# Moving the load of the decay floors' logits to the end of the first tile's chains of loads and remainders

## Chip, cores and metric

The kernel runs on one core of a Trainium2 chip. The metric is the device time of one execution in microseconds (us). The change concerns a stretch of some 40 us at the start of an execution of about 1.86 ms.

A core has a matrix engine (TensorE, PE in the profile; its weight loads are shown apart as PEld), a vector engine (VectorE, DVE), a scalar engine (ScalarE, ACT), GpSimd (POOL) and SyncE (SP), which here issues most of the DMA transfers. Each of them works through its own list of instructions in order. Where an instruction has to wait, all that stands behind it in that list waits too.

## The reference

A decoder trunk of two layers over 512 tokens of width 1024. Each layer adds three branches to the residual stream x:

```python
for l in range(DEPTH):
    x = x + 0.5 * swiglu(rms_norm(x, ffn1_norm[l]), ffn1_w_in[l], ffn1_w_out[l])
    h = rms_norm(x, mix_norm[l]) @ w_mix_in[l]
    ...
    x = x + y @ w_mix_out[l]      # y: short convolution, HGRN2 and forgetting attention side by side
    x = x + 0.5 * swiglu(rms_norm(x, ffn2_norm[l]), ffn2_w_in[l], ffn2_w_out[l])
```

The HGRN2 heads of the middle branch have a learned lower bound (floor) for their decay. The floors of both layers come from a softmax over the layers of a small array of logits, 2 x 256 numbers:

```python
lb_soft = jax.nn.softmax(hgrn_lb_logits.astype(jnp.float32), axis=0)
lower_bounds = jnp.clip(jnp.cumsum(lb_soft, axis=0) - lb_soft[0:1], 0.0, 1.0)
```

The floors are first needed in layer 0's middle branch, whose first instruction that reads them (L1201) starts 373.2 us into the profiled execution.

## The kernel before

**Products in three passes.** Every float32 operand is split into a high part (`hi`), written by ACT as a rounded copy, and a remainder (`lo`), which DVE computes as the operand less its high part. A product is three matmuls: high by high, high by remainder, remainder by high.

**The opening** (`open_stream`, L1546 to L1649) is the first tile of the first feed-forward branch: columns 0 and 1 of the gate and of the up projection, so four accumulators, over eight slices j of 128 input features, taken in pairs k = 0, 2, 4, 6. For each slice:

- `load(j)` (L1554) has SP fetch 256 KB of x into `xs`; `weights(k)` (L1572) has SP fetch 512 KB of weights for a pair of slices into `st`, of which there are two buffers. So the weights of k = 4 can only be issued when those of k = 0 have been split.
- `turn(j)` (L1562) turns the slice with four PE transposes into a PSUM bank.
- `norm_part(j, ..., 0)` multiplies by the norm's gain: ACT writes the high part of the activations (L381), DVE the remainder (L382).
- `part` (L1579) splits the weights: ACT the high part (L1581), DVE the remainder (L1582).
- `product` (L1625) issues the matmuls, twelve for each slice: four accumulators by three passes.
- The bank is copied to the residual stream by DVE (L1647), and squares are summed for the norm, by ACT (L392, L395) and DVE (L396).

For k = 0 the twelve products of slice 0 come first, then those of slice 1, accumulator by accumulator. Slices 2 and 3 are turned between the two groups.

**What sets the order.** The builder arranges the instructions of each engine by itself, by priority and by its own estimate of when each can run. Where the kernel wants a certain order it calls `follow(engine, instruction)` (L273). This keeps one chain for each engine, "p" (PE), "a" (ACT), "v" (DVE), "s" (SP) and "g" (POOL), and adds a dependence on the last instruction in the chain, which costs no semaphore but fixes which of the two comes first on their engine. In the opening all loads are in chain "s" (two are in ACT's "a"), all high parts in "a", all remainders in "v", all transposes and products in "p". What is not in a chain is placed by the builder wherever it sees room.

**After the opening**, in `cover` (L481), come `build_consts` (masks, by DVE at L231 to L241; the builder pulls much of this forward into the opening), the sum of squares through PE (`end_norm`, L408) with its logarithm, exponential and square on ACT (L413, L414 and L401, all shown as L267, the line of the helper `act`) and three steps on DVE (L402 to L404), then `lower_bounds` (L918), the procedure that the change touches. It fetches the logits (L930), copies the first layer's row (L932), takes the maximum (L934), subtracts it (L937), has ACT take the exponential (L938, shown as L267 on tile lb), normalises, sums and clips (L940 to L967) and has ACT take a logarithm (L970). ACT then loads another table of functions (L258), which waits in ACT's list behind all of these.

The second tile (f = 2) follows at once. Its weights are fetched by L287, whose instructions are in chain "s", behind the loads of the opening, and split at L304 (ACT) and L305 (DVE). Its fourth accumulator is the bank that `end_norm` has used.

Of the kernel before, what the change touches and what calls it, by code (L numbers as in the profile page):

```python
# [23 lines left out]
P = 128  # L24
# [132 lines left out]
class Trunk:  # L157
# [760 lines left out]
    def lower_bounds(self, logits, scratch):  # L918
        nc = self.nc
        used = 0  # L920

        def take(*shape):
            nonlocal used
            n = shape[0] * (shape[1] if len(shape) > 1 else 1)
            t = scratch[:, used : used + n]
            used += n
            return t.rearrange("p (l r) -> p l r", r=2) if len(shape) > 1 else t

        lg = take(DEPTH, 2)
        nc.sync.dma_start(lg, logits.rearrange("l (r p) -> p l r", p=P))  # L930
        m = take(2)
        nc.vector.tensor_copy(m, lg[:, 0, :])  # L932
        for l in range(1, DEPTH):
            nc.vector.tensor_max(m, m, lg[:, l, :])  # L934
        e = take(DEPTH, 2)
        for l in range(DEPTH):
            nc.vector.tensor_sub(e[:, l, :], lg[:, l, :], m)  # L937
        self.act(e, e, AF.Exp)  # L938
        s = take(2)
        nc.vector.tensor_copy(s, e[:, 0, :])  # L940
        for l in range(1, DEPTH):
            nc.vector.tensor_add(s, s, e[:, l, :])
        nc.vector.reciprocal(s, s)
        for l in range(DEPTH):
            nc.vector.tensor_mul(e[:, l, :], e[:, l, :], s)
        self.lb = self.const.tile([P, DEPTH, 2], F32, tag="lb", name="lb")

        self.lb1 = self.const.tile([P, DEPTH, 2], F32, tag="lb1", name="lb1")
        cum = take(2)
        nc.vector.tensor_copy(cum, e[:, 0, :])  # L950
        for l in range(DEPTH):
            if l:
                nc.vector.tensor_add(cum, cum, e[:, l, :])
            d = take(2)
            nc.vector.tensor_sub(d, cum, e[:, 0, :])
            nc.vector.tensor_scalar(
                self.lb[:, l, :], d, scalar1=0.0, scalar2=1.0, op0=ALU.max, op1=ALU.min
            )
            nc.vector.tensor_scalar(
                self.lb1[:, l, :], self.lb[:, l, :], scalar1=-1.0, scalar2=1.0,  # L960
                op0=ALU.mult, op1=ALU.add,
            )
        one = take(DEPTH, 2)
        nc.vector.tensor_scalar(
            one, self.lb1, scalar1=0.0, scalar2=-1e30, op0=ALU.is_equal, op1=ALU.mult
        )
        nc.vector.tensor_scalar(  # L967
            self.lb1, self.lb1, scalar1=2.0**-40, scalar2=None, op0=ALU.max
        )
        self.act(self.lb1, self.lb1, AF.Ln)  # L970
        nc.vector.tensor_add(self.lb1, self.lb1, one)
# [729 lines left out]
```

## Time and profile before

| | |
|---|---|
| timed runs, median of 3 | 1856.22 us |
| lowest and highest timed run | 1854.98 and 1859.03 us |
| the profiled execution's own time | 1863.95 us |
| its span in the trace | 1862.1 us |
| PE busy | 1842.6 us, 99% of the span |
| DVE, ACT, POOL busy | 1480.4, 1003.3, 177.4 us |
| DMA traffic | 251.91 MB, mean 135 GB/s |

The profiled execution is one single execution, recorded instruction by instruction. The timeline lists instructions with their start, their duration, and in brackets how long their engine had been idle before them and what ended that wait. Consecutive like instructions are merged into one row with their count (x5). Durations of consecutive instructions overlap a little, since an engine starts one before the end of the last is recorded; the distance between starts is then the pace. The chain of waits goes back from the end and shows at each point of time what the end depended on. The granted clock of PE is a column in the views by stretches of time: 1.00 is full speed.

### The profile page before, as it was taken

The numbers are of one execution on the slowest core, as the hardware profiler recorded it, in microseconds if no ns is written. First come the engines' busy times: TensorE is split into PE (matmuls) and PEld (weight loads), VectorE is DVE, ScalarE is ACT, GpSimd is POOL, SyncE is SP. The second block draws the span as 40 slices with busy tenths as digits, with TensorE's granted clock in tenths as the row PEclk, the third lists the DMA queues.
The fourth block names the chain that finished last, engine by engine and source line by source line (L and its number), as shares of the span: only waits on it lengthen the run. The fifth ranks groups of instructions, "written<-read, shape, count | busy, mean of one in ns | idle before, by whom it ended". The sixth has DMA issues, their size and how long they took to land.

```text
span 1862.1 us, 33406 instructions
## 1 busy us (share of the span) xinstructions
PE 1842.6 (99%) x13551; PEld 1712.6 (92%) x13551; DVE 1480.4 (80%) x2102; ACT 1003.3 (54%) x1465; POOL 177.4 (10%) x182
## 2 busy tenths in 40 slices
PE   8999999999999999999999999999999999999998
PEld 7899999899878899999889999998998788999997
DVE  8889787677887888878678887876768878888883
ACT  5455554564675454545445555555546665555552
POOL 0011120100000001112001111201000000021210
PEclk9999999999999999999999999999999999999999
DMA  5858783332323756868265787823323238577662
GB/s 162 212 121 195 176 179 91 74 93 69 80 80 93 213 134 156 183 168 171 80 194 132 163 178 188 166 69 76 90 68 86 76 97 226 146 156 197 147 138 91
DMA packets 244427, 251.91 MB, mean 135 GB/s; under 512 B 18569, under 2 KB 229009, under 8 KB 244273
## 3 DMA queue, kind: packets, MB, share of 16 engines
q1 hardware_dynamic: 190512, 183.56, 32.7%
q0 software_dynamic: 53600, 66.09, 22.3%
q8 instruction: 106, 1.74, 0.4%
q14 instruction: 49, 0.39, 0.1%
q10 hardware_dynamic: 160, 0.14, 0.0%
HBM read 223.98 MB, written 2.10 MB: 121 GB/s over the span
## 4 chain that ended last, share of the span: by engine, by line
PE 89%; DVE 6%; ACT 2%; issue 1%; DMA 1%; SPq 0%; ACTq 0%; DVEq 0%
PE mm L315 13%; PE mm L322 13%; PE mm L321 13%; PE sc L322 6%; PE sc L315 6%; PE sc L321 6%; PE pt L315 6%; PE pt L321 6%; PE pt L322 6%; PE po L315 3%; PE po L322 3%; PE po L321 3%; PE po L1477 1%; PE pt L1518 1%; DVE hl L305 1%
## 5 line engine op out<-in xcount | busy, mean ns | idle before, releaser
L771 ACT CAST hl<-w 128x1024 fp32r<-128x1024 f32 x322 | 337.1, 1049 | 327.6 <-PE mm L322 77.2
L773 DVE TENSOR_TENSOR hl<-w,hl 128x1024 fp32r<-128x1024 f32 x322 | 392.8, 1222 | 93.2 <-ACT hl L771 93.0
L305 DVE TENSOR_TENSOR hl<-st,hl 128x512 fp32r<-128x512 f32 (+2 forms) x188 | 161.4, 859 | 115.3 <-ACT hl L304 114.3
L304 ACT CAST hl<-st 128x512 fp32r<-128x512 f32 (+2 forms) x188 | 142.0, 755 | 184.3 <-PE mm L322 70.7
L315 PE MATMUL mm<-xc,hl 128*128 128x256 f32 (+1 forms) x732 | 202.3, 277 | 1.8 <-ACT g L877 1.4
L321 PE MATMUL mm<-xc,hl 128*128 128x256 f32 x728 | 202.0, 277 | 0.0
L322 PE MATMUL mm<-xc,hl 128*128 128x256 f32 x728 | 202.0, 277 | 0.0
L315 PE MATMUL sc<-xc,hl 128*128 128x256 f32 (+1 forms) x530 | 147.1, 278 | 2.5 <-ACT g L877 1.7
L322 PE MATMUL sc<-xc,hl 128*128 128x256 f32 x528 | 146.8, 278 | 0.0
L321 PE MATMUL sc<-xc,hl 128*128 128x256 f32 x528 | 146.7, 278 | 0.0
L315 PEld LDWEIGHTS mm<-xc,hl 128*128 128x128 f32 x732 | 137.3, 188 | 2.5 <-ACT g L877 1.8
L321 PEld LDWEIGHTS mm<-xc,hl 128*128 128x128 f32 x728 | 137.4, 189 | 0.0
L322 PEld LDWEIGHTS mm<-xc,hl 128*128 128x128 f32 x728 | 136.7, 188 | 0.1
L315 PE MATMUL pt<-xc,hl 128*128 128x256 f32 (+1 forms) x484 | 133.6, 277 | 0.0
L321 PE MATMUL pt<-xc,hl 128*128 128x256 f32 x480 | 133.4, 278 | 0.0
L322 PE MATMUL pt<-xc,hl 128*128 128x256 f32 x480 | 133.2, 278 | 0.0
L315 PE MATMUL mm<-hl,x 128*128 128x256 f32 (+1 forms) x384 | 112.3, 293 | 0.7 <-DVE qk L1408 0.3
L315 PE MATMUL mm<-x,hl 128*128 128x512 f32 x272 | 109.3, 402 | 0.0
L322 PE MATMUL mm<-hl,x 128*128 128x256 f32 (+1 forms) x384 | 107.4, 280 | 0.0
L321 PE MATMUL mm<-hl,x 128*128 128x256 f32 (+1 forms) x384 | 107.2, 279 | 0.0
L322 PE MATMUL mm<-x,hl 128*128 128x512 f32 x272 | 106.9, 393 | 0.0
L321 PE MATMUL mm<-x,hl 128*128 128x512 f32 x272 | 106.0, 390 | 0.0
(490 smaller groups left out, 5689.8 us busy)
## 6 DMA issues: line engine op xcount, KB each, us to landing
w<-in_ffn_w_in_dram SPq DMA_DIRECT2D x140, 512.0 KB, 5.3
w<-in_ffn_w_out_dram SPq DMA_DIRECT2D x64, 512.0 KB, 4.5
w<-in_ffn_w_out_dram POOLq DMA_DIRECT2D x56, 512.0 KB, 8.7
st<-in_w_mix_in_dram SPq DMA_DIRECT2D x88, 256.0 KB, 2.7
st<-in_ffn_w_in_dram SPq DMA_DIRECT2D x70, 256.0 KB, 3.5
w<-in_ffn_w_in_dram POOLq DMA_DIRECT2D x35, 512.0 KB, 8.7
w<-S POOLq DMA_DIRECT2D x35, 512.0 KB, 4.7
st<-in_ffn_w_out_dram SPq DMA_DIRECT2D x24, 512.0 KB, 3.5
```

The costliest lines, as they stand in the source:

```text
L304: a = nc.scalar.copy(hi, src[:, c : c + w])
L305: b = nc.vector.tensor_sub(lo, src[:, c : c + w], hi)
L315: i = nc.tensor.matmul(acc[:, c], ah, bh[:, c], start=first and c.start == 0, stop=False, skip_group_check=True,)
L321: nc.tensor.matmul(acc, ah, bl, start=False, stop=False, skip_group_check=True)
L322: i = nc.tensor.matmul(acc, al, bh, start=False, stop=last, skip_group_check=True)
L771: A(nc.scalar.copy(hi, src))
L773: return lambda: V(nc.vector.tensor_sub(lo, src, hi))
L1477: nc.tensor.matmul(self.ob[:, t0 + u * P : t0 + 2 * P], V[:, j, h % 4].rearrange("p a d -> p (a d)"), part[:, j, u:, :].rearrange("p i t - ...
L1518: nc.tensor.transpose(tb[:, j * P : (j + 1) * P], p[:, j * P : (j + 1) * P], self.ident)
```

## The change

```diff
         lg = take(DEPTH, 2)
-        nc.sync.dma_start(lg, logits.rearrange("l (r p) -> p l r", p=P))
+        self.follow("s", nc.sync.dma_start(lg, logits.rearrange("l (r p) -> p l r", p=P)))
         m = take(2)
-        nc.vector.tensor_copy(m, lg[:, 0, :])
+        self.follow("v", nc.vector.tensor_copy(m, lg[:, 0, :]))
         for l in range(1, DEPTH):
             nc.vector.tensor_max(m, m, lg[:, l, :])
```

When `lower_bounds` is called, the last link of chain "s" is the load of the opening's last pair of weights (k = 6), and the last link of chain "v" is the weight remainder of slice 7. So the transfer of the logits is placed on SP behind all loads of the opening, and the copy on DVE behind all its remainders. The steps that read the copy's result (L934 on) come later with it. What joins the two chains afterwards, the loads of the second tile first of all, comes behind them. No instruction is added or taken away, and nothing that is computed changes.

## Prediction

> **What bounds the kernel now.** I read the page's engine table first, then the chain of waits over the opening.
>
> ```profile
> span 1862.1 us, 33406 instructions
> PE 1842.6 (99%) x13551; PEld 1712.6 (92%) x13551; DVE 1480.4 (80%) x2102; ACT 1003.3 (54%) x1465; POOL 177.4 (10%) x182
> ```
>
> ```profile
> 7.68 4.87 DMA lb<-in_hgrn_lb_logits_dram
> ...
> 13.98 2.67 PE sc L1625 x5
> 16.65 2.56 PE pt L1625 x6
> 19.21 1.75 PE sc L1625 x6
> 20.96 1.37 PE pt L1625 x6
> 22.32 0.87 PE mm L1562 x8
> ```
>
> PE sets the time nearly everywhere. The exception is early: from 7.68 us the end depends on a transfer of 2 KB, the logits. The timeline of DVE, then of PE, shows who stood behind it.
>
> ```profile
> 8.16 0.22 DVE L231 TENSOR_SCALAR c<-c 128x128 f32<-128x128 f32 x1
> 12.57 0.17 DVE L932 COPY lb<-lb 128x2 f32<-128x2 f32 x1 [4.20 <-DMA lb<-in_hgrn_lb_logits_dram]
> 12.65 0.28 DVE L233 TENSOR_TENSOR c<-c,c 128x128 f32<-128x128 f32 x1
> 12.85 0.15 DVE L934 TENSOR_TENSOR lb<-lb 128x2 f32<-128x2 f32 x1
> 12.97 0.29 DVE L234 TENSOR_TENSOR lmask<-c,c 128x128 uint8<-128x128 f32 x1
> 13.18 0.74 DVE L382 SCALAR_TENSOR_TENSOR x<-mm,gain,x 128x512 fp32r<-128x512 f32 x1
> 13.84 0.68 DVE L1582 TENSOR_TENSOR hl<-st,hl 128x512 fp32r<-128x512 f32 x1
> ...
> 16.57 0.68 DVE L1582 TENSOR_TENSOR hl<-st,hl 128x512 fp32r<-128x512 f32 x1
> ```
>
> ```profile
> 10.47 0.48 PE L1625 MATMUL sc<-x,hl 128*128 128x512 f32 x1
> 13.98 0.80 PE L1625 MATMUL sc<-x,hl 128*128 128x512 f32 x1 [3.03 <-DVE x L382]
> ```
>
> DVE stands still for 4.20 us at the copy L932. Slice 1's activation remainder (L382) is behind it, and PE has done one of slice 1's twelve products and waits for that remainder. The pause has a second cost, which the stretches of half a microsecond show (columns: stretch, its length, PE, PEld, DVE, ACT, POOL busy, granted PE clock, DMA share, GB/s):
>
> ```profile
> 12.00:12.50 0.50, 0.00 (x0) 0.00 (x0) 0.00 (x0) 0.00 (x0) 0.00 (x0) 1.00 0.16 1
> 13.00:13.50 0.50, 0.00 (x0) 0.00 (x0) 0.50 (x3) 0.00 (x0) 0.00 (x0) 0.54 0.00 0
> 19.00:19.50 0.50, 0.50 (x3) 0.40 (x2) 0.50 (x2) 0.35 (x1) 0.00 (x0) 0.50 0.55 162
> 20.00:20.50 0.50, 0.50 (x4) 0.41 (x3) 0.50 (x2) 0.41 (x1) 0.00 (x0) 1.00 0.96 252
> ```
>
> PE's last product before the pause ends at 10.95. From about 13.0 the granted clock is 0.50, and it is 1.00 again only after 19.5. Products done meanwhile run at half pace.
>
> **The change, part by part.** *The pause removed.* The chain's row at 20.96, at full clock, gives the pace: six products in 1.37 us, 0.23 each. After the product at 10.47 the next could start at 10.70; it started at 13.98. That is **3.28 us**. *The half clock removed.* The chain's three pieces from 13.98 on are 17 products in 2.67 + 2.56 + 1.75 = 6.98 us; at 0.23 they take 3.91. That is **3.07 us**. Together 6.35, if nothing else is late.
>
> What is late next? ACT's part of slice 1 (timeline of ACT) is early:
>
> ```profile
> 8.02 0.69 ACT L381 ACTIVATE x<-mm,gain 128x512 fp32r<-128x512 f32 x1 [1.72 <-PE mm L1562]
> 8.61 0.61 ACT L1581 CAST hl<-st 128x512 fp32r<-128x512 f32 x1
> ```
>
> L382 can start at 8.71; if DVE fills in L233 and L234 first, at about 8.9. So DVE's list moves up by 13.18 - 8.9 = 4.3 us, and ends slice 1's weight remainder near 10.2 (14.52 before). PE needs these at 10.70 and 10.93, both there. Slice 2: PE arrives at 10.70 + 11 x 0.23 = 13.2 and needs the weight remainder at 13.7; it was ready at 17.25, so now near 12.95. Slice 3 comes after twelve products (2.76) and the transposes (0.87 at 22.32), from 16.8; its two large DVE steps follow those of slice 2 and have 3 us more. The smallest margin is 0.7 us; an order of DVE that puts one more operation of 0.7 us ahead costs nothing, a second one its length. The later slices hang on PE's own transposes, and move with PE.
>
> Do the transfers keep up? The row at 12.00 shows 1 GB/s: all that had been issued has landed, the x slices 4 and 5 included, which PE now turns at 16.0. The remaining loads wait on SP for buffers, not for the wire:
>
> ```profile
> 14.55 0.88 SPq L1572 DMA_DIRECT2D st<-in_ffn_w_in_dram  x2
> ...
> 18.54 0.88 SPq L1572 DMA_DIRECT2D st<-in_ffn_w_in_dram  x2
> 26.16 13.97 SPq L287 DMA_DIRECT2D st<-in_ffn_w_in_dram  x8
> ```
>
> The weights of slices 4 and 5 (14.55) waited for slice 1's remainder, ended 14.52; so they go near 10.3, and those of 6 and 7 (18.54) some 4.3 earlier too. Slice 4 is turned at 22.32 and multiplied after that, so its weights had 7.8 us or more from their issue. They now go 4.3 earlier and are wanted 6.3 earlier, which leaves 5.8. The longest landing of this stretch that I have quoted, behind a full queue, is the logits' 4.87.
>
> *The transfer moved.* It is one issue on SP. It stood at 7.68, after which SP waited until 14.55 anyway, and goes behind the row of 18.54, which ends at 19.42, ahead of the row of 26.16: SP has 6.7 us there and pays nothing. It landed 4.87 after issue behind a full queue; issued near 15 it is there by 20. The copy cannot run before slice 7's weight remainder, which ends at 34.2 (33.55 + 0.68) in the next rows, near 27.9 when 6.3 are taken off. So the copy finds its data, unless the transfer takes 13 us.
>
> *The copy and what follows it.* L932 and L934 (0.32 together) leave a pause and enter a busy stretch of DVE. Then comes the one place without slack:
>
> ```profile
> 33.55 0.68 DVE L1582 TENSOR_TENSOR hl<-st,hl 128x512 fp32r<-128x512 f32 x1
> ...
> 35.35 0.16 DVE L940 COPY lb<-lb 128x2 f32<-128x2 f32 x1
> ...
> 36.21 0.69 DVE L396 TENSOR_TENSOR sqa<-sqa,sq 128x512 f32<-128x512 f32 x1
> ```
>
> ```profile
> 40.51 0.19 ACT L267 ACTIVATE lb<-lb 128x4 f32<-128x4 f32 x1
> 40.64 0.63 ACT L267 ACTIVATE nr<-nr 128x512 f32<-128x512 f32 x1
> ```
>
> ```profile
> 42.71 0.19 PEld L315 LDWEIGHTS po<-x,hl 128*128 128x128 f32 x1 [0.40 <-DVE nt L402]
> ```
>
> The floors' logarithm (40.51) stands on ACT ahead of the norm's exponential (40.64) and square; L402 on DVE takes the square; PE's fourth accumulator of the second tile waits for L402, already 0.40. If the floors come x later, PE waits up to x more. Lower bound 0: from 34.2 the copy, maximum and exponential fit before L940 at 35.35. Upper bound, if DVE takes its larger steps first: the copy goes behind L396, which ends at 36.9 (36.21 + 0.69), 1.55 after L940's old place. I take **0.35**, near the lower end, since the copy's turn comes with the next gap of DVE. Sum: 6.35 - 0.35 = **6.0 us**.
>
> The profiled execution would have a span of 1862.1 - 6.0 = 1856.1 and a time of 1857.95, as 1.85 lay around its span before. Its own time is 7.73 above the median of the runs, so I subtract from the median: 1856.22 - 6.0 = **1850.2**, with 1848.5 to 1852 for this case alone: 1.2 more for the full 1.55 on the floors and 0.6 for one margin overdrawn; the other way the 0.35, and up to 1.3 for the waits on DVE inside the slow pieces of the chain, which shrink too.
>
> The Trainium skill ("TensorE: Matmul & The Clock Gate", Part 1: The HAM clock gate) says that PE falls to half clock after an idle window of about 3.4 us and recovers after about 3.4 us of busy work, in a window that runs freely. By that rule the half clock would cost about 1.7 us and the sum would be near 4.6; the rows show the clock down after some 2 us of pause and for more than 6 us, so they don't agree in length, and the rows are what I use.
>
> **Rivals.** *The pause does not cost the clock in timed runs.* The profile is slower than the median by more than I expect to win, and may hold a slow stretch that they lack. Then only 3.28 - 0.35 = 2.9 is won: 1853.3. For it: those 7.73 us, and that the pause is short, 3.03. Against: the pause follows from an order, which all runs share. By the freely running window of the Trainium skill ("TensorE: Matmul & The Clock Gate", Part 1) it would be a matter of chance in each execution; one profile can't show that.
>
> *The floors come late (slower).* Place: ACT's list ahead of the norm. If the builder puts the exponential there while DVE does the copy only behind the second tile's third weight remainder:
>
> ```profile
> 40.05 1.23 DVE L305 TENSOR_TENSOR hl<-st,hl 128x1024 fp32r<-128x1024 f32 x1 [0.35 <-ACT hl L304]
> ```
>
> then the floors start from 41.28, need 0.6 to the exponential and the 5.16 from 35.35 to 40.51: 47.0, 6.5 late. PE pauses 6.5, and pays the 3.07 of half clock again: 9.6 - 6.35 = 3.2 slower, 1859.4. It decides from a lateness of 6.35 - 3.07 = 3.3. Against: L940 ran at 35.35 between two large steps, and the copy can do so too.
>
> *The builder arranges later stages differently.* Every moved estimate can change its choices.
>
> ```profile
> 42.00:1862.10 1820.10, 1805.27 (x13392) 1682.31 (x13390) 1447.42 (x2002) 982.68 (x1430) 176.34 (x174) 1.00 0.56 135
> ```
>
> PE idles 14.8 us in all the rest. Twice that costs 14.8 - 6.0 = 8.8: 1865; it decides from 6.0. A third less wins 5 more: 1845. For it: the middle branches have few chains. Against: that idle time is small and scattered.
>
> *It does not do what it says:* another wait ends the same pause, 1856. Only slice 1's inputs could, and their rows are early.
>
> **How the numbers follow.** Forecast 0.55; clock rival 0.15; late floors 0.05; other arrangement 0.22 (0.08 better, 0.04 in between, 0.10 worse); no effect 0.03. With 0.2% (3.7 us, about what a measurement tells from no change): faster 0.55 + 0.08 + 0.05 of the clock rival = 0.68; slower 0.10 + 0.02 = 0.12; same 0.20. The range, 1846.5 to 1857.5, leaves out most of the worse arrangements and late floors (0.13) and the best arrangements (0.05).
>
> **What would show it.** In the profile after: no idle row of 4 us on DVE before L932; L382 of slice 1 near 8.9; PE without a pause from 6.4 to 40 and a granted clock of 1.00 from 10 to 20; twelve products in about 2.8 us; the transposes of slices 4 and 5 near 16 instead of 22.32; the fourth accumulator's first product near 36.7 instead of 42.71; 14.8 us of idle PE later as before. It is wrong if PE pauses near 11 for something else, if the clock is at half with no pause, or if the 6 us are won by 40 us and gone at the end.

## The result and the profile after

| | before | after |
|---|---|---|
| timed runs, median | 1858.03 us (22 runs) | 1853.42 us (22 runs) |
| lowest and highest | 1853.8 and 1863.9 | 1849.17 and 1860.92 |
| ratio of after to before | | 0.9974, 95% interval 0.9962 to 0.9985 |
| second measurement (e12 below) | 1859.16 us (12 runs) | 1852.91 us (7 runs), ratio 0.9964, 0.9947 to 0.9982 |
| span of the profiled execution | 1862.1 us | 1853.6 us |

The change makes the kernel faster, by 0.26% in the first measurement and 0.36% in the second. The forecast of 6.0 us is a ratio of 0.9968, inside both intervals. But 4.6 us between the first medians, 6.2 between the second, and 8.5 between two profiled spans are three different answers, and single runs of one kernel spread over 10 us. (One of the twelve runs of e5 below took 3720.07 us, twice the others, for a reason that nothing here shows; it stands in no ratio.) So the opening is read by a mark inside it: the start of **the first product of the second tile's fourth accumulator** (L315 on tile po), 42.71 us before.

The chain of waits of the changed kernel, over the stretch that was shown of before (start, duration, what):

```profile
10.30 0.44 PE po L1562 x4
10.74 1.39 PE sc L1625 x6
12.13 1.36 PE pt L1625 x6
13.49 1.36 PE sc L1625 x6
14.85 1.36 PE pt L1625 x6
16.21 0.87 PE mm L1562 x8
```

The transfer of the logits is gone from it, and PE goes through without a break. Slices 4 and 5 are turned from 16.21 instead of 22.32: 6.11 us earlier. The 18 products of the three pieces from 10.74 take 4.11, so 17 take 3.88 where they took 6.98: 3.10 us are the slow products, and the other 3.01 are the pause. (By the starts in the timeline of PE the second product of slice 1 comes at 10.81 instead of 13.98, so 3.17 are the pause, and some 2.93 are left for the products; the expectations below use this split.) The timeline of DVE after shows why:

```profile
8.16 0.22 DVE L231 TENSOR_SCALAR c<-c 128x128 f32<-128x128 f32 x1
8.41 0.29 DVE L233 TENSOR_TENSOR c<-c,c 128x128 f32<-128x128 f32 x1
8.73 0.29 DVE L234 TENSOR_TENSOR lmask<-c,c 128x128 uint8<-128x128 f32 x1
8.94 0.75 DVE L382 SCALAR_TENSOR_TENSOR x<-mm,gain,x 128x512 fp32r<-128x512 f32 x1
9.61 0.68 DVE L1582 TENSOR_TENSOR hl<-st,hl 128x512 fp32r<-128x512 f32 x1
```

The copy L932 has left its place between L231 and L233. Slice 1's remainder L382 starts at 8.94 (13.18 before). SP's list and the norm's steps on ACT (timelines), and the mark:

```profile
14.31 0.88 SPq L1572 DMA_DIRECT2D st<-in_ffn_w_in_dram  x2
15.23 0.47 SPq L930 DMA_DIRECT2D lb<-in_hgrn_lb_logits_dram  x1
20.04 7.18 SPq L287 DMA_DIRECT2D st<-in_ffn_w_in_dram  x3
```

```profile
34.53 0.20 ACT L267 ACTIVATE lb<-lb 128x4 f32<-128x4 f32 x1
34.64 0.62 ACT L267 ACTIVATE nr<-nr 128x512 f32<-128x512 f32 x1
```

```profile
36.70 0.50 PE L315 MATMUL po<-x,hl 128*128 128x512 f32 x1
```

The mark comes at 36.70, 6.01 us earlier. Of the 6.11 won by 16.21 us only 0.10 is lost on the way to it.

### The profile page after: what moved, and what is told of

Read it like the earlier page. It is cut to its first block, busy times and chain, and to the rows that moved or that the text cites. A ratio compares the mean times of both kernels' runs of the same rounds, so it can differ in the third digit from the quotient of the medians.

```text
span 1853.6 us, 33407 instructions
## 1 busy us (share of the span) xinstructions
PE 1836.2 (99%) x13551; PEld 1707.7 (92%) x13551; DVE 1480.4 (80%) x2102; ACT 1002.6 (54%) x1465; POOL 177.3 (10%) x182
## 4 chain that ended last, share of the span: by engine, by line
PE 90%; DVE 6%; ACT 3%; issue 1%; DMA 0%; ACTq 0%; DVEq 0%
PE mm L315 13%; PE mm L322 13%; PE mm L321 13%; PE sc L322 6%; PE sc L315 6%; PE sc L321 6%; PE pt L315 6%; PE pt L321 6%; PE pt L322 6%; PE po L315 3%; PE po L321 3%; PE po L322 3%; PE po L1477 1%; PE pt L1518 1%; DVE hl L305 1%
## 5 line engine op out<-in xcount | busy, mean ns | idle before, releaser
L315 PE MATMUL mm<-xc,hl 128*128 128x256 f32 (+1 forms) x732 | 201.6, 276 | 1.8 <-ACT g L877 1.4
L315 PE MATMUL sc<-xc,hl 128*128 128x256 f32 (+1 forms) x530 | 147.1, 278 | 2.5 <-ACT g L877 1.7
L315 PEld LDWEIGHTS mm<-xc,hl 128*128 128x128 f32 x732 | 137.2, 188 | 2.5 <-ACT g L877 1.8
L315 PE MATMUL pt<-xc,hl 128*128 128x256 f32 (+1 forms) x484 | 133.6, 277 | 0.0
L315 PE MATMUL mm<-hl,x 128*128 128x256 f32 (+1 forms) x384 | 112.6, 293 | 1.3 <-DVE zf L1073 0.6
L315 PE MATMUL mm<-x,hl 128*128 128x512 f32 x272 | 109.2, 402 | 0.0
```

The source lines that it names most:

```text
L315: i = nc.tensor.matmul(acc[:, c], ah, bh[:, c], start=first and c.start == 0, stop=False, skip_group_check=True,)
```

## The experiments

**e1 and e2: each half of the change alone.**

```diff
 e1
-        nc.vector.tensor_copy(m, lg[:, 0, :])
+        self.follow("v", nc.vector.tensor_copy(m, lg[:, 0, :]))
 e2
-        nc.sync.dma_start(lg, logits.rearrange("l (r p) -> p l r", p=P))
+        self.follow("s", nc.sync.dma_start(lg, logits.rearrange("l (r p) -> p l r", p=P)))
```

> Only the copy is in its chain; the transfer stays where it was, early on SP. The mark is the first product of the second tile's fourth accumulator (42.71 us before, 36.70 with the whole change). Theory (what counts is what stands behind the copy on DVE): mark 36.7, no pause of PE, granted clock 1.00 from 10 to 20 us, time as with the whole change, about 5 to 6 us under before. Rival (the early transfer itself holds up the loads behind it on SP or in the queue): the mark stays over 38.

> Only the transfer is in its chain; the builder places the copy by its own estimate, which comes out behind slice 5's remainders. Theory: the copy finds its data there, mark 36.7 and time as with the whole change. Rival (the builder's estimate of the landing is too early here as well): DVE waits 1 to 4 us before the copy near 23 us, and the mark lies between 37.5 and 41.

Measured: e1 1851.24 us against 1858.71, ratio 0.9951 (0.9931 to 0.9972); e2 1852.58, ratio 0.9965 (0.9946 to 0.9984). The marks, e1 first:

```profile
36.86 0.50 PE L315 MATMUL po<-x,hl 128*128 128x512 f32 x1 [0.15 <-DVE nt L402]
```

```profile
36.68 0.50 PE L315 MATMUL po<-x,hl 128*128 128x512 f32 x1
```

Either half alone does what both do. In e1 the transfer is still issued early, and holds up nobody: only the copy's place on DVE matters. In e2 the builder knows that the transfer is late and puts the copy behind slice 5's remainders by itself, where it does not wait (timeline of DVE, e2):

```profile
22.86 0.22 DVE L232 TENSOR_SCALAR c<-c 128x128 f32<-128x128 f32 x1
23.00 0.16 DVE L932 COPY lb<-lb 128x2 f32<-128x2 f32 x1
23.12 0.29 DVE L233 TENSOR_TENSOR c<-c,c 128x128 f32<-128x128 f32 x1
```

e1 shows one more thing. The floors' logarithm starts at 34.69 in it, 0.16 later than after the whole change, and the mark is 0.16 later:

```profile
34.69 0.21 ACT L267 ACTIVATE lb<-lb 128x4 f32<-128x4 f32 x1
34.80 0.62 ACT L267 ACTIVATE nr<-nr 128x512 f32<-128x512 f32 x1
```

So the place without slack that the prediction named is real: there, lateness of the floors goes one for one into PE.

**e4, e6, e7: the pause brought back without the logits.** All have the whole change, and fillings on DVE in the place of the old wait (ten, six and fourteen).

```diff
-        zeros = fp.tile([P, T], F32, tag="u2", name=self.n("z"), bufs=2)[:, :P]
+        wide = fp.tile([P, T], F32, tag="u2", name=self.n("z"), bufs=2)
+        zeros = wide[:, :P]
...
                     turn(1)
+                    for _ in range(10):
+                        V(nc.vector.memset(wide, 0.0))
                     make(1)
```

> The whole change, with ten fillings of a 128x512 tile with zeros added on DVE ahead of slice 1's activation remainder, about 4.4 us of DVE's time where the wait was. No logits are involved. Theory: the old pause comes back with its half clock, PE pauses 3.2 us, the mark is 42.7 to 42.9, the time as before. Rival (the half clock came from the stretch of DMA traffic or was chance): PE pauses 3.2 us, but the clock stays at 1.00 and the mark is 39.9.

> The whole change with six fillings on DVE ahead of slice 1's activation remainder (ten gave a pause of 4.13 us on PE, 0.66 each). Theory (the clock falls only after a pause of some length): pause 1.5, clock 1.00 throughout, mark 36.70 + 1.5 = 38.2. Rival (each microsecond of pause costs its share of clock too, 6.1 us for 3.17): mark 39.6.

> The same with fourteen fillings. Theory (the clock falls once, whatever the length, and comes back after the same time of work): pause 6.8, half clock until some 6 us after the pause, mark between 36.70 + 6.8 + 1.5 = 45.0 and 36.70 + 6.8 + 2.93 = 46.4. Rival (cost in proportion to the pause, 6.1 us for 3.17): mark 49.8.

PE at the pause and at the mark (timeline of PE, where the products' line is L1626; a fence for each, in the order e6, e4, e7):

```profile
12.54 1.79 PE L1626 MATMUL sc<-x,hl 128*128 128x512 f32 x5 [1.59 <-DVE x L382]
...
39.02 0.50 PE L315 MATMUL po<-x,hl 128*128 128x512 f32 x1
```

```profile
15.24 2.67 PE L1626 MATMUL sc<-x,hl 128*128 128x512 f32 x5 [4.13 <-DVE x L382]
...
43.75 0.50 PE L315 MATMUL po<-x,hl 128*128 128x512 f32 x1
```

```profile
17.92 2.67 PE L1626 MATMUL sc<-x,hl 128*128 128x512 f32 x5 [6.97 <-DVE x L382]
...
46.25 0.50 PE L315 MATMUL po<-x,hl 128*128 128x512 f32 x1
```

A filling, with the step that the builder put behind most of them, took 0.66 us and not 0.44, so e4's pause is longer than planned. The granted clock stayed at 1.00 in e6. In e4 and e7 it fell and came back as these stretches show (last columns: clock, DMA share, GB/s; e4, then e7):

```profile
12.00:14.00 2.00, 0.00 (x0) 0.00 (x0) 1.79 (x7) 0.76 (x2) 0.00 (x0) 0.89 0.00 0
14.00:16.00 2.00, 0.76 (x2) 0.46 (x2) 1.91 (x5) 0.00 (x0) 0.00 (x0) 0.50 0.00 0
20.00:20.50 0.50, 0.50 (x3) 0.40 (x2) 0.50 (x2) 0.26 (x1) 0.00 (x0) 0.63 0.91 275
```

```profile
15.00:16.00 1.00, 0.00 (x0) 0.00 (x0) 0.94 (x4) 0.00 (x0) 0.00 (x0) 0.84 0.00 0
16.00:18.00 2.00, 0.08 (x1) 0.08 (x1) 1.85 (x6) 0.00 (x0) 0.00 (x0) 0.50 0.00 0
22.00:23.00 1.00, 1.00 (x5) 0.72 (x5) 1.00 (x3) 0.09 (x1) 0.00 (x0) 0.75 0.77 226
```

A mean of 0.89 over two microseconds is half clock for the last 0.44 of them, so from 13.56; 0.63 over half a microsecond puts its end at 20.37. For e7 the same reading gives 15.68 to 22.50. Both stretches are 6.8 us long. From 10.8, where slice 1's second product started after the whole change, e4 resumes 4.4 late and then works 20.37 - 15.24 = 5.1 us at half pace, which costs 2.6: 36.70 + 7.0 = 43.7, measured 43.75. e7 resumes 7.1 late and works 4.6 us at half pace: 36.70 + 9.4 = 46.1, measured 46.25. So **the cost is the pause plus half of the time that PE works in the half-clock stretch**, to 0.15, and no multiple of the pause: e7's pause is more than twice that of before and e7 pays less for the clock. e6 comes 2.3 late for 1.7 of late resumption, and no clock. Of its further 0.6, 0.5 is a second wait on DVE: its next product starts only at 13.14, when slice 1's weight remainder (L1582, 12.41 + 0.68) is done, and the one behind it at 13.47, 0.93 after the resumption instead of 0.46. The time of e4 is that of before (ratio 0.9999, 0.9983 to 1.0015), though no logits stand in the way.

**e3, e5, e9: the pause kept, the clock kept up.** The kernel before, with products of zeros for PE to work on during the pause.

```diff
+                if k == 0 and i == 13:
+                    for _ in range(27):
+                        E(nc.tensor.matmul(
+                            jobs[0][0][:, :P], zeros, zeros, start=False, stop=False,
+                            skip_group_check=True,
+                        ))
                 product(*what)
```

> The kernel before, with 27 products of zeros added on PE into the first accumulator, between the first and the second product of slice 1, so that PE has work during the pause. DVE still waits 4.2 us for the logits. Theory (half of the gain is the clock): slice 1's second product still starts near 14.0, the granted clock stays 1.00, the mark is 42.71 - 2.93 = 39.8, and the time 2.9 us under before. Rival (the slow products are slow for another reason, such as DVE's or the loads' lateness): mark 42 to 43, time as before.

> The warm pause with half the filling: in e3 each of the 27 calls made two passes on PE, so the work lasted 5.94 us and outlasted the pause by 2.75. Thirteen calls should end at 13.7, inside the pause. Theory (2.93 us of the gain is the clock): slice 1's second product starts near 14.0, the clock stays 1.00, the mark (42.71 before) is 39.8, and the time 2.9 us under before. Rival (the products after the pause are slow for another reason): mark 42 to 43.

> e5 once more, with the floors' subtraction (L937) put in DVE's chain behind the opening's remainders, because in e5 the builder moved the floors' whole chain ahead of slice 4's remainder and DVE was late there. The copy and its wait stay early. Theory (the clock costs 2.9 us after the pause): second product of slice 1 near 14.2, clock 1.00, mark 40.0 to 40.6 (42.71 before, less 2.93, plus the 0.3 that the filling outlasts the pause and some lateness of DVE). Rival (DVE, 4.3 us late, bounds this stretch whatever the clock): mark 42 to 43.

e3 missed its aim (16.73 instead of 14.0 for the second product; mark 44.80), and so did e5 (14.29, then the floors' chain in the way; mark 42.89); their ratios, 0.9987 (0.9973 to 1.0002) and 0.9994 (0.9978 to 1.0010), tell little. e9 keeps the clock up through the pause. Its timelines of PE, of DVE and of ACT, and last the turn of slice 4 in the kernel before (timeline of PE):

```profile
14.21 1.57 PE L1625 MATMUL sc<-x,hl 128*128 128x512 f32 x5
...
19.77 1.03 PE L1562 MATMUL mm<-ident,xs 128*128 128x128 f32 x8
...
23.39 2.30 PE L1625 MATMUL sc<-x,hl 128*128 128x512 f32 x6
...
41.73 0.50 PE L315 MATMUL po<-x,hl 128*128 128x512 f32 x1
```

```profile
12.58 0.17 DVE L932 COPY lb<-lb 128x2 f32<-128x2 f32 x1 [4.21 <-DMA lb<-in_hgrn_lb_logits_dram]
...
21.64 0.29 DVE L233 TENSOR_TENSOR c<-c,c 128x128 f32<-128x128 f32 x1
...
22.89 0.29 DVE L234 TENSOR_TENSOR lmask<-c,c 128x128 uint8<-128x128 f32 x1
23.10 0.74 DVE L382 SCALAR_TENSOR_TENSOR x<-mm,gain,x 128x512 fp32r<-128x512 f32 x1
```

```profile
20.41 0.69 ACT L381 ACTIVATE x<-mm,gain 128x512 fp32r<-128x512 f32 x1
```

```profile
22.16 1.04 PE L1562 MATMUL mm<-ident,xs 128*128 128x128 f32 x8
```

DVE waits as before, PE keeps its full clock (1.00), and slice 4 is turned at 19.77 instead of 22.16. From slice 1's second product to that turn PE took 8.18 us before (13.98 to 22.16), takes 5.56 here (14.21 to 19.77), and 5.24 after the whole change (10.81 to 16.05). So **some 2.5 us of the slow products are the clock** (2.39 by the turn, 2.62 by the stretches), and the rest is remainders that come late at full clock too, as in e6.

At the mark (41.73) only 0.98 us of the gain is left, between what the two theories said. From slice 4's turn to the mark e9 takes 1.41 more than before (21.96 against 20.55). PE has gone through the 35 products of slices 1 to 3 that were left and arrives at slice 4 at 23.39, whose remainder starts only at 23.10, so these six products take 2.30 instead of about 1.5. The rest is lost near 31.7, on a chain of waits that goes back to the same place (slice 5's weight remainder on DVE at 25.10, the load L287 at 25.73, its splitting on ACT at 29.52). DVE's lateness alone doesn't hold slice 4's remainder up: ACT's part of it is done at 21.10, and DVE has done at 21.61 all that stands ahead of it in the kernel before. But in e9's list six mask steps (L231 to L234) come first, from 21.64 to 23.10; in the kernel before they stand behind it, and DVE is idle for 1.93 us at that place. By an estimate from these rows the mark would be 41.73 - 1.41 = 40.3 without them; no run had this order. So e9 shows the clock's share as far as slice 4's turn, and **how much of it would reach the mark with DVE's order unchanged is not shown**.

**e8, e10: the kernel before, unchanged; e11, e12: the changed kernel, unchanged.**

> The kernel before, unchanged, for one more profile. Theory A (the pause always costs the clock): DVE waits 4.2 us for the logits, PE pauses 3.0, half clock for 6.8 us, mark 42.7. Theory B (it depends on where the pause falls in the clock's own rhythm): the same pause, but half clock for another length, 0 or 3.4 us, and a mark of 39.8 or 41.3. Span between 1851 and 1866 us, in steps of some 4.3 us by how many of the later feed-forward branches run their matmuls at 117.8 instead of 113.3 ns.

> The kernel before, unchanged, a third profile. The stretch of half clock was 6.83 us long in the first and 3.41 in the second. Theory (the clock's rhythm isn't tied to the kernel): again 0, 3.41 or 6.83 us, and a mark of 39.8 to 42.7, the later the longer the stretch. Rival (6.83 is the rule and the second one an exception): mark 42.7.

> The changed kernel, unchanged, a second profile. Theory: no pause, so nothing for the rhythm to act on after the opening's first products; mark 36.7 if the clock comes up by 6.5 us, up to 37.4 if it comes up as late as in the second profile of before (7.95). Any other mark would speak against it. The later branches at 113.3 or 117.8 ns by chance, span 1847 to 1860.

> The changed kernel, unchanged, timed once more against the kernel before in five rounds. Theory (5.2 to 6.3 us won in the opening, nothing given back): ratio 0.9966 to 0.9972, mark 36.7 to 36.9 in its profile. Rival (some of it is given back later, as the first ratio of 0.9974 may hint): ratio 0.998 or more.

The marks of before are 42.71, then in e8 and e10:

```profile
42.03 0.50 PE L315 MATMUL po<-x,hl 128*128 128x512 f32 x1 [0.18 <-DVE nt L402]
```

```profile
43.05 0.50 PE L315 MATMUL po<-x,hl 128*128 128x512 f32 x1 [0.15 <-DVE nt L402]
```

Those of the changed kernel are 36.70, 36.80 (e11) and 36.75 (e12). In e8 the same pause cost less:

```profile
13.90 2.45 PE L1625 MATMUL sc<-x,hl 128*128 128x512 f32 x5 [2.23 <-DVE x L382]
16.15 2.49 PE L1625 MATMUL pt<-x,hl 128*128 128x512 f32 x6
18.47 1.55 PE L1625 MATMUL sc<-x,hl 128*128 128x512 f32 x6
```

```profile
14.50:15.00 0.50, 0.50 (x2) 0.42 (x3) 0.50 (x2) 0.00 (x0) 0.00 (x0) 0.78 0.00 0
18.00:18.50 0.50, 0.50 (x4) 0.40 (x3) 0.50 (x2) 0.00 (x0) 0.00 (x0) 0.81 0.77 206
```

Its half clock lasts from 14.78 to 18.19, 3.4 us, and begins only after PE has resumed. In e10 it lasts from 13.38 to 20.20, 6.8 us, as in the first profile:

```profile
13.00:13.50 0.50, 0.00 (x0) 0.00 (x0) 0.50 (x2) 0.00 (x0) 0.00 (x0) 0.88 0.00 0
20.00:20.50 0.50, 0.50 (x4) 0.39 (x3) 0.50 (x2) 0.40 (x1) 0.00 (x0) 0.80 0.67 221
```

So the size of the clock term is a matter of the execution. How often it is large can be read from the timed runs, each of which has its mean granted clock on record, to three places. Half clock for 6.8 us of 1860 takes 0.0018 off it (the first profile and e10 have 0.998), for 3.4 us 0.0009 (e8 has 0.999). Of 58 timed runs of before, beside e1, e5 and e12, 10 have 0.998, 42 have 0.999 and 6 have 1.000; of 29 of the changed kernel 25 have 1.000 and 4 have 0.999. The clock can also be low in the last two microseconds, which blurs the third place, and the times don't sort by it, as the spread described next is larger; but **the short stretch is the common one, and the long one, from which the prediction took its 3.07 us, the rarer**. By the marks, the opening wins between 5.2 us (42.03 less 36.80) and 6.4 (43.05 less 36.70).

The rest of the spread lies elsewhere. The same 20 us of a later feed-forward branch (layer 1, first) in e8, e10, e1 and e2, a fence each; the number to read is PE's count in brackets:

```profile
1040.00:1060.00 20.00, 20.00 (x172) 20.00 (x171) 15.21 (x17) 9.57 (x12) 3.53 (x3) 1.00 0.62 124
```

```profile
1040.00:1060.00 20.00, 20.00 (x179) 20.00 (x178) 15.85 (x17) 10.32 (x13) 3.52 (x3) 1.00 0.61 118
```

```profile
1040.00:1060.00 20.00, 20.00 (x179) 20.00 (x178) 17.03 (x18) 10.57 (x12) 4.72 (x4) 1.00 0.94 186
```

```profile
1040.00:1060.00 20.00, 20.00 (x172) 20.00 (x172) 16.15 (x17) 10.48 (x13) 4.81 (x4) 1.00 0.67 133
```

e8 and e10 are one kernel, and run this stretch at 172 or 179 products (those cut by its ends included), both at a granted clock of 1.00. e1 and e2 have marks 0.18 us apart and spans 8.0 us apart (1849.4 and 1857.4).

## Why the prediction was right, point by point

- **The pause (3.28 predicted).** Right: 3.01 by the chain, 3.17 by the starts. L382 was forecast near 8.9 and started at 8.94, the transposes of slice 4 near 16 and started at 16.21, the mark near 36.7 and came at 36.70. e4 shows that the wait on DVE is a sufficient cause, with no transfer in it; e1 that the transfer's place isn't one.
- **The half clock (3.07 predicted).** Right for the profile it was taken from, 3.10, of which by e9 some 2.5 are the clock itself. As a term it was taken for fixed, and the runs show it isn't: the stretch is 6.8 us in two profiles of before and 3.4 in the third, and by the clocks on record about 3.4 in most timed runs. The rival in which timed runs don't pay the clock was half right: most pay less than the 3.07, and the 6 with 1.000 had no such stretch.
- **The two terms as a sum.** Right for the profiles, with DVE's list moved up by 4.2 (L382 from 13.18 to 8.94; 4.3 predicted). That the mark came 6.01 earlier where 6.0 was forecast is luck in part: the pause was forecast 0.27 too large and the floors' loss 0.25 too large, and the two cancel. And 6.0 is the gain over a profile with the long stretch of half clock; over e8 the mark is 5.3 earlier.
- **The floors' lateness (0.35, between 0 and 1.55).** The place is right and so is the rate, in the one case seen (e1: 0.16 for 0.16). The size was too large: all that is lost between 16.21 and the mark is 0.10. The copy went to 29.21, right behind the last copy to the residual stream.
- **The transfer on SP.** Right: issued at 15.23, 4.8 us ahead of L287, at no cost.
- **The rivals.** Late floors and a costly new arrangement didn't happen: outside the opening only the order of a handful of instructions near 28 to 34 us changed, the rest of each engine's list is the same. "It does not do what it says" falls with the mark.
- **The time.** 1850.2 was forecast from a median of three runs, 1856.22; 22 runs of before have 1858.03, and 1858.03 - 6.0 = 1852.0 stands against 1853.42 measured. The median of before was low by 1.8; single runs spread over 10 us, so three are too few for it, though what paces (below) those three had is not on record. The range for this case alone, 1848.5 to 1852, was missed by 1.4; moved up by the same 1.8 it holds 1853.42.

What stays open: the average timed gain. The two intervals allow both 5.2 and 6.4; the clocks on record speak for a value near 5.2, as the short stretch is the common one. That nothing is given back later rests on the unchanged lists and on a comparison where the paces of the branches happen to be the same: the last sum of squares through PE (L408, timeline of PE) starts at 1542.03 in the profile of before and at 1535.98 in that of e2, whose lists are the same outside the opening too, 6.05 us earlier, and the first at 38.73 and 32.70, 6.03 earlier.

## What to carry to other kernels

A tiny transfer costs what stands behind its first reader in that engine's list, so pin the reader behind the urgent work of its engine; the place of the transfer itself mattered little here. Read a pause of PE with the granted clock beside it: in the first profile the clock about doubled its price, in most runs it added less. Keeping the clock up with idle products won 2.4 us by the turn of slice 4, and by an estimate a new order of DVE's list took 1.4 of it back by the mark, so look for such moves before a gain or a loss is put down to the clock. Where single executions spread more than the gain, compare a mark inside the trace over several profiles, not two spans.

## What was not expected of the hardware

- Pauses of 1.59 us (e6) and 1.76 us (e5, at 23.62) of PE left the granted clock at 1.00; pauses of 2.23 to 6.97 us all lowered it to half, for 3.4 or 6.8 us, whatever the pause's length. It was 6.8 in the four profiles in which the clock fell during the pause, and 3.4 in e8, where it fell after PE had resumed. The Trainium skill ("TensorE: Matmul & The Clock Gate", Part 1: The HAM clock gate) speaks of an idle window of about 3.4 us and a window that runs freely. The freely running part and the unit of 3.4 agree: behind the same wait the clock of the kernel before fell at 13.04, 14.78 and 13.38, for 3.4 us or twice that. The length of idle time doesn't: in the first profile it fell after about 2.1 us of pause (10.95 to 13.04).
- The later feed-forward branches ran many of their 256-column products at 117.8 instead of 113.3 ns (26.5 or 25.5 us for 225 of them) at a granted clock of 1.00, for up to 130 us, some 4.3 us a branch. It struck layer 0's second branch and either of layer 1's in no fixed pattern: in two, two and one of them in the three profiles of before, in one each in the three of after, in none in e1 and two in e2. What sets it was not tried.
